# A decoder trunk in fp32: paired matmuls issued as a group, a planner with more rules, another step order, and one ratio per row in the differential softmax

## The chip, the cores and the metric

The kernel runs on one core of one Trainium2 chip. The metric is device time in microseconds (us). Engines are named as in the profile: PE is TensorE (matmuls), PEld its weight load, DVE is VectorE, ACT is ScalarE, POOL is GpSimd, SP issues the DMAs.

## What is computed

Two layers of a decoder on one sequence of 256 tokens, width 1024. Layer 0 mixes tokens by causal attention with 16 heads of 64 (its block size is 256, so the one block is the whole sequence and nothing is selected). Layer 1 uses differential attention: 8 heads, each with two score matrices and values of width 128. Behind each mixer stands an MLP of width 4096 with a squared ReLU. Each of the four sub-layers is modulated by a conditioning vector c and closed with a layer norm.

```python
mod = einsum('bd,lde->lbe', silu(c), ada_w) + ada_b
for i in range(2):
    shift1, scale1, gate1, shift2, scale2, gate2 = split(mod[i], 6)
    h = x * (1 + scale1) + shift1
    y = causal_attention(h) if i == 0 else diff_attention(h)
    x = layer_norm(ALPHA * x + (1 + gate1) * y)
    h = x * (1 + scale2) + shift2
    x = layer_norm(ALPHA * x + (1 + gate2) * (square(relu(h @ w_up[i])) @ w_down[i]))

# diff_attention, per head: s has two components, causal mask
p = softmax(s)                      # over keys
w = p[0] - lam * p[1]
o = rms_norm(w @ v, subln_g) * (1 - lambda_init)
```

## The kernel before

The 256 tokens are two blocks of 128 (b = 0, 1). All weights are read once, about 158 MB, on SP's queue. Every dense product is made of three matmuls in a rounded fp32 format: each weight tile `raw` is split into `hi` (ACT, L484) and `lo = raw - hi` (DVE, L485), each activation likewise, and PE adds hi·hi, hi·lo and lo·hi (L521 to L523, L538). There are three `raw` buffers of 1 MB, and eight `hi` and eight `lo` pieces.

The conditioning products stand on DVE: `aw`, 128 rows of `ada_w`, is loaded into one of two buffers and multiplied with silu(c) and summed in one instruction (L563), 96 times.

Attention goes by calls for two head pairs at a time (g = 0 to 3) and a block of queries b: 8 calls a layer. A scores call (`scores`, L783) takes two PSUM banks of the tag `sc`, of which there are two. Its matmuls contract over 64 rows, so each uses one row half of PE's array (64x128), and the two components `cpt` of a pair use the two halves. A call has 4 such matmuls for b = 0 and 8 for b = 1. The profile has two records for each. `softmax` masks on DVE and takes the exponential on ACT (L752). In layer 0 ACT scales each probability tile by its reciprocal sum (L847), PE transposes it (L765), ACT copies it out (L767), and the values matmuls (`attend_values_T`, L852) use the two column halves of the array (128x64). In layer 1 the second component is scaled on ACT by -lam over its sum (L805), DVE combines both (L806), and the values matmuls (L823) use the whole array. The RMS norm then scales the result on DVE (L834).

What sets the order: `PROGRAM` lists the steps (a: one conditioning row block; q, v, o, u, d: weight loads; V, Q: projections; T: transposes of queries and keys; S: a scores call with softmax; P: a values call; O: output projection; C: close with a norm; U, X, Y, D: MLP). Each step adds its instructions to one list. `Planner.forward` then goes through that list with its own costs per instruction and puts each engine's instructions in an order: of those it holds to be ready on the engine that is free first, it takes the one that stands earliest in the list.

```python
lim = t + wait_ns
pick = min([x for x in c if x[2] <= lim])
```

A scores or values matmul (`pairable`) may be followed at once by the next of the list if that is ready within 60 ns. `issue_in_order` fixes the result: each engine issues strictly in that order.

Of the kernel before, what the change touches and what calls it, by code (L numbers as in the profile page):

```python
# [15 lines left out]
F32 = mybir.dt.float32  # L16
F32R = mybir.dt.float32r
AF = mybir.ActivationFunctionType
ALU = mybir.AluOpType
# [26 lines left out]
    Q001 V000 a031 a037 a030 T001 Q000 Q011 S02 a024 a042 a022 q02 a021 T011 S03 a025 Q010 T010 T000 V010 S01  # L46
    a020 S00 Q002 T002 a044 a035 q03 S04 P02 a034 P01 P03 Q012 Q003 a046 a026 Q013 v01 a033 V011 V001 P00 a043
    P04 a045 T003 a023 S06 T012 S05 T013 S07 P06 a027 P05 G00 P07 K01 o00 O000 a040 a041 a047 o01 O001 a036 O010
    a032 N00 C000 O011 C010 u00 U000 u01 U001 X000 K00 a114 R010 u02 d00 a115 a126 a100 a113 a056 R000 a120 a121
    u04 d01 a124 U011 a110 u03 a101 a116 D000 d02 X001 a132 a053 a104 a112 a102 X011 a125 a050 U010 a137 a052  # L50
    a103 X010 a136 Y02 D001 D010 u06 a055 Y03 a151 a122 a106 d03 a051 D002 D003 a105 D011 d04 u07 Y04 u05 D004
    D012 Y06 a107 Y05 a145 D013 a111 a117 Y07 D014 a135 a142 d05 d07 a054 a133 d06 D015 D005 D006 a057 G01 D007
    N01 a156 C001 q10 D016 D017 C011 q11 Q100 T100 Q101 Q110 Q111 a141 q13 Q103 T110 S11 v10 T103 a131 a134 T101
    a123 a153 S12 T111 S10 Q113 a127 V100 P12 a143 a140 V110 a155 q12 S13 P10 F10 Q112 P11 F11 T113 a146 R011
    a154 F12 Q102 T102 o11 a144 T112 S14 S16 a150 S17 a130 v11 V111 P13 V101 P14 F13 G10 o10 P16 S15 F14 P17
    a147 R001 a152 F16 P15 F17 F15 O100 N10 O101 C100 u10 O110 O111 C110 U100 u11 u12 u13 d12 d10 X100 U101 u14
    D100 X101 d11 U110 a157 U111 K11 X110 D110 X111 u16 Y13 D111 u15 Y12 Y14 Y16 D112 K10 d14 d13 D113 d16 D101
    D102 D103 D104 u17 D114 d15 R110 Y15 G11 Y17 D105 D106 d17 D107 R100 C101 D115 E1 C111
# [110 lines left out]

class Planner:  # L170
# [3 lines left out]
    def __init__(self, ins, slots, psum_names, cost=_cost):  # L174
# [3 lines left out]
        self.costs = [cost(i, eng[k], psum_names) for k, i in enumerate(ins)]  # L178
# [51 lines left out]
    def forward(self, prio, wait_ns=0.0):  # L230
# [12 lines left out]
        dma = 0.0  # L243
        start, end = [0.0] * N, [0.0] * N
        orders = [[] for _ in range(5)]
        lastpe = -1

        def met(k, t):
            need[k] -= 1
# [921 lines left out]
```

## Time and profile before

| | |
|---|---|
| time, median of 3 runs | 650.22 us (648.86 to 650.66) |
| profiled execution | 649.94 us, its span 647.8 us |
| PE busy / DVE / ACT | 615.0 / 498.6 / 387.4 us |
| HBM read | 156.62 MB, 243 GB/s over the span |
| granted TensorE clock, mean | 0.994 |

Rows of the profile are read like this: a group row has line, engine, operation, out<-in, shapes and count, then busy us and mean ns of one, then the idle time of the engine just before and what ended it. A timeline row has start, duration and instruction. A wait row has who waited for whom, us in total, times and the longest. A row of a stretch has its bounds and length, busy time of each engine with the number of instructions, granted clock, share of the DMA engines and GB/s. Matmuls overlap in the pipeline and their ends are modelled, so a busy PE is not PE at its peak.

### The profile page before, as it was taken

The numbers are of one execution on the slowest core, as the hardware profiler recorded it, in microseconds if no ns is written. First come the engines' busy times: TensorE is split into PE (matmuls) and PEld (weight loads), VectorE is DVE, ScalarE is ACT, GpSimd is POOL, SyncE is SP. The second block draws the span as 40 slices with busy tenths as digits, with TensorE's granted clock in tenths as the row PEclk, the third lists the DMA queues.
The fourth block names the chain that finished last, engine by engine and source line by source line (L and its number), as shares of the span: only waits on it lengthen the run. The fifth ranks groups of instructions, "written<-read, shape, count | busy, mean of one in ns | idle before, by whom it ended". The sixth has DMA issues, their size and how long they took to land.

```text
span 647.8 us, 8858 instructions
## 1 busy us (share of the span) xinstructions
PE 615.0 (95%) x3148; PEld 498.2 (77%) x3148; DVE 498.6 (77%) x899; ACT 387.4 (60%) x731; POOL 27.7 (4%) x36
## 2 busy tenths in 40 slices
PE   4989999999999999999989999999999999999995
PEld 3767767776887787777877878788788888888884
DVE  5899779889979778788869979787885455646457
ACT  3547875787745463647446678686786556555530
POOL 0000000011000000000011002012100000000001
PEclk9999989999999999999999999999999999999998
DMA  8999857888979979798957757740767356555301
GB/s 292 409 344 378 303 181 257 296 266 276 321 243 383 311 247 365 269 365 314 323 178 273 253 189 271 250 165 31 252 206 253 135 194 195 196 191 180 148 0 66
DMA packets 66086, 158.25 MB, mean 244 GB/s; under 512 B 4057, under 2 KB 21370, under 8 KB 66042
## 3 DMA queue, kind: packets, MB, share of 16 engines
q1 hardware_dynamic: 66042, 157.68, 69.0%
q8 instruction: 25, 0.41, 0.2%
q14 instruction: 19, 0.16, 0.1%
HBM read 156.62 MB, written 1.05 MB: 243 GB/s over the span
## 4 chain that ended last, share of the span: by engine, by line
PE 58%; DMA 16%; DVE 15%; issue 4%; ACT 4%; POOL 2%; SPq 0%; DVEq 0%; ACTq 0%; POOLq 0%
PE ac L538 11%; DMA aw<-in_ada_w_dram 11%; PE sc L538 9%; PE mm L522 5%; PE mm L521 5%; PE mm L523 5%; DVE lo L485 5%; DVE aw L563 4%; PE mm L1069 4%; PE tp L1069 4%; DMA raw<-in_moba_w_in_dram 3%; PE sc L783 3%; ACT hi L484 2%; PE tp L1074 2%; PE mm L1074 2%
## 5 line engine op out<-in xcount | busy, mean ns | idle before, releaser
L485 DVE TENSOR_TENSOR lo<-raw,hi 128x1024 fp32r<-128x1024 f32 x196 | 231.0, 1198 | 61.4 <-ACT hi L484 59.9
L484 ACT CAST hi<-raw 128x1024 fp32r<-128x1024 f32 x196 | 199.4, 1034 | 109.2 <-PE sc L538 37.8
L563 DVE CUSTOM_DVE_ANT_0 aw<-aw,sbc,tabT 128x1024 f32<-128x1024 f32 x96 | 121.9, 1281 | 27.0 <-DMA aw<-in_ada_w_dram 26.9
L521 PE MATMUL mm<-hi,hT 128*128 128x512 f32 x224 | 91.2, 409 | 3.9 <-ACT hi L484 3.0
L522 PE MATMUL mm<-lo,hT 128*128 128x512 f32 x224 | 90.5, 405 | 0.7 <-DVE lo L485 0.7
L523 PE MATMUL mm<-hi,hT 128*128 128x512 f32 x224 | 89.4, 400 | 0.2 <-DVE hT L662 0.2
L1069 PE MATMUL mm<-hT,hi 128*128 128x512 f32 x192 | 61.3, 398 | 0.2 <-ACT hi L484 0.2
L1069 PE MATMUL tp<-hT,hi 128*128 128x512 f32 x192 | 61.0, 395 | 0.0
L538 PE MATMUL ac<-lo,sTh 128*128 128x512 f32 x160 | 50.9, 398 | 3.8 <-DVE lo L485 3.8
L521 PEld LDWEIGHTS mm<-hi,hT 128*128 128x128 f32 x224 | 42.6, 190 | 14.1 <-ACT hi L484 3.7
L538 PE MATMUL ac<-hi,sTh 128*128 128x512 f32 x160 | 50.7, 397 | 1.5 <-ACT hi L484 1.5
L538 PE MATMUL ac<-hi,sTl 128*128 128x512 f32 x160 | 51.2, 397 | 0.0
L522 PEld LDWEIGHTS mm<-lo,hT 128*128 128x128 f32 x224 | 42.7, 190 | 10.4 <-DVE lo L485 2.1
L523 PEld LDWEIGHTS mm<-hi,hT 128*128 128x128 f32 x224 | 42.6, 190 | 9.6 <-DVE hT L662 0.8
L538 PE MATMUL sc<-hi,sTl 128*128 128x512 f32 x144 | 45.8, 394 | 1.4 <-DVE sTl L1086 1.4
L538 PE MATMUL sc<-hi,sTh 128*128 128x512 f32 x144 | 46.2, 395 | 0.0
L538 PE MATMUL sc<-lo,sTh 128*128 128x512 f32 x144 | 45.8, 392 | 0.0
L1074 PEld LDWEIGHTS tp<-hT,lo 128*128 128x128 f32 x192 | 34.5, 188 | 7.5
L1074 PEld LDWEIGHTS mm<-hT,lo 128*128 128x128 f32 x192 | 34.2, 188 | 7.6 <-DVE lo L485 0.5
L538 PEld LDWEIGHTS ac<-lo,sTh 128*128 128x128 f32 x160 | 29.3, 188 | 11.7 <-DVE lo L485 5.9
L1074 PE MATMUL tp<-hT,lo 128*128 128x256 f32 x192 | 36.9, 279 | 0.0
L1074 PE MATMUL mm<-hT,lo 128*128 128x256 f32 x192 | 36.6, 280 | 0.1
(173 smaller groups left out, 898.2 us busy)
## 6 DMA issues: line engine op xcount, KB each, us to landing
aw<-in_ada_w_dram SPq DMA_DIRECT2D x96, 512.0 KB, 5.7
raw<-in_mlp_w_up_dram SPq DMA_DIRECT2D x32, 1024.0 KB, 6.3
raw<-in_mlp_w_down_dram SPq DMA_DIRECT2D x32, 1024.0 KB, 5.6
raw<-in_diff_w_in_dram SPq DMA_DIRECT2D x16, 512.0 KB, 5.2
raw<-in_moba_w_in_dram SPq DMA_DIRECT2D x24, 256.0 KB, 6.8
raw<-in_moba_w_in_dram SPq DMA_DIRECT2D x8, 512.0 KB, 6.0
raw<-in_moba_w_out_dram SPq DMA_DIRECT2D x4, 1024.0 KB, 4.9
raw<-in_diff_w_in_dram SPq DMA_DIRECT2D x4, 1024.0 KB, 5.4
```

Of the source, the lines that this page charges most:

```text
L484: act.copy(out=hi[:, :n], in_=raw_ap)
L485: vec.tensor_tensor(out=lo[:, :n], in0=raw_ap, in1=hi[:, :n], op=ALU.subtract)
L521: pe.matmul(dst, lhsT=xh, rhs=wh, start=start, stop=False)
L522: pe.matmul(dst, lhsT=xh, rhs=wl, start=False, stop=False)
L523: pe.matmul(dst, lhsT=xl, rhs=wh, start=False, stop=stop)
L538: pe.matmul(dsts[h], lhsT=a, rhs=w[:, h * 512:(h + 1) * 512], start=start and k == 0 and i == 0, stop=stop and k == n - 1 and i == 2)
L563: vec.tensor_tensor_reduce(out=aw, in0=aw, in1=sbc, scale=1.0, scalar=adab_cols(l, v)[:, j:j + 1], op0=ALU.mult, op1=ALU.add, accum_out=dst)
L783: pe.matmul(r[i, cpt][:, kb * P:(kb + 1) * P], lhsT=qk[l, b, g][rows, i, :], rhs=qk[l, kb, g][rows, 2 + i, :], start=True, stop=True)
L1069: pe.matmul(ps, lhsT=w[k][0][:, c_], rhs=x3[k], start=first, stop=last)
L1074: pe.matmul(ps[:, 0:S], lhsT=w[k][1][:, c_], rhs=x3[k][:, 0:S], start=False, stop=False)
```

## The change

The matmuls of one scores call, and of one values call in layer 0, get a group number. The planner starts a group only when everything that it needs from outside is there, and then issues nothing else on PE until the group is through. PE's costs in the planner depend on the kinds of a matmul and of the one before it (whole array, row half, column half). A transfer that starts near the end of the one before gets an extra delay in the planner. The backward pass, which was not called, goes. `PROGRAM` has another order of steps. In layer 0 a values call scales its four probability tiles first and then makes all transposes. In layer 1 the second component is no longer scaled on ACT: DVE adds it with the ratio -lam·sum0/sum1 per row, and the first sum goes into the RMS norm's factors.

```diff
 PROGRAM = """
-    Q001 V000 a031 a037 a030 T001 Q000 Q011 S02 a024 a042 a022 q02 a021 T011 S03 a025 Q010 T010 T000 V010 S01
+    Q000 a020 V000 a046 v01 V010 Q001 a100 a043 V011 a024 a036 T000 S00 a032 Q010 a023 a045 q02 P00 a040 a025
...
+def _kind(i):
+
+    t = tuple(i.tile_size)
+    if t == (128, 128):
+        return int(not i.is_transpose and "float32r" in str(i.ins[0].dtype))
+    return (2 if t[0] < 128 else 4) + int(any(i.tile_position))
...
+    def gap(self, x, paired, y):
+
+        a, b = self.kind[x], self.kind[y]
+        if a < 2:
+            return self.costs[x][0] + (92 if b >= 2 else 0), 0
+        if a // 2 == b // 2:
+            return 111 if a != b or paired else 223, 0
+        return 209 if paired else 313, (55, 105)[b] if b < 2 else 0
...
+            if not inside:
+                todo[g] -= 1
+                opened[g] = max(opened.get(g, 0.0), t)
+                if todo[g] == 0:
+                    for m in members[g]:
+                        if need[m] == 0:
+                            cand[4].append((m, opened[g]))
+                    return
...
-            pick = None
-            if e == 4 and pair[lastpe] and lastpe + 1 < N and pair[lastpe + 1]:
-                for x in c:
-                    if x[1] == lastpe + 1 and x[2] <= t + 60:
-                        pick = x
-            if pick is None:
-                lim = t + wait_ns
-                pick = min([x for x in c if x[2] <= lim])
+            if e == 4 and last is not None and togo.get(group[last]):
+                c = [x for x in c if group[x[0]] == group[last]]
+            pick = min([x for x in c if x[1] <= t])
...
-                dma = max(s + 1530, dma) + self.bytes_[k]
-                end[k] = dma + 1150
+                x = s + 1530 - dma
+                x = 850 if -1000 <= x <= 1000 else 230 if -2500 <= x < -1000 else 0
+                dma = max(s + 1530, dma) + self.bytes_[k] + x
+                end[k] = dma + 800
...
-    return o.ap[0][1] * _elems(o) / r / 16 * (8 + r * 4 * 0.0368) * 1.03
+    return o.ap[0][1] * _elems(o) / r / 16 * (8 + r * 4 * 0.0368)
...
+    @contextmanager
+    def together():
+        n = len(nc.cur_bb.bb.instructions)
+        yield
+        for i in nc.cur_bb.bb.instructions[n:]:
+            groups[i.name] = n
...
-        for i in range(2):
-            for kb in range(b + 1):
-                for cpt in (1, 0):
...
+        with together():
+            for i in range(2):
+                for kb in range(b + 1):
+                    for cpt in (1, 0):
...
-            ws = []
+            sums = small.tile([P, 4], F32, tag="sums2", name="sums2", bufs=3)
+            inv = small.tile([P, 4], F32, tag="inv", name="inv", bufs=3)
+            tt = small.tile([P, 4], F32, tag="tt", name="tt", bufs=3)
+            p1, p2 = ([softmax(b, sc[i, cpt], sums, 2 * cpt + i) for i in range(2)] for cpt in range(2))
+            vec.reciprocal(out=inv, in_=sums)
+            vec.scalar_tensor_tensor(out=tt[:, 0:2], in0=inv[:, 2:4], scalar=nlam, in1=sums[:, 0:2],
+                                     op0=ALU.mult, op1=ALU.mult)
             for i in range(2):
-                sums = small.tile([P, 2], F32, tag="sums2", name="sums2", bufs=4)
-                p1 = softmax(b, sc[i, 0], sums, 0)
-                p2 = softmax(b, sc[i, 1], sums, 1)
-                vec.reciprocal(out=sums, in_=sums)
-                vec.tensor_tensor(out=sums[:, 1:2], in0=sums[:, 1:2], in1=nlam, op=ALU.mult)
-                act.activation(out=p2[:, :n], in_=p2[:, :n], func=AF.Copy, scale=sums[:, 1:2])
-                vec.scalar_tensor_tensor(out=p1[:, :n], in0=p1[:, :n], scalar=sums[:, 0:1], in1=p2[:, :n],
+                vec.scalar_tensor_tensor(out=p1[i][:, :n], in0=p2[i][:, :n], scalar=tt[:, i:i + 1], in1=p1[i][:, :n],
                                          op0=ALU.mult, op1=ALU.add)
-                ws.append(p1)
-            probs[kind, b, g] = ws, None
+            vec.tensor_scalar(out=tt[:, 2:4], in0=inv[:, 0:2], scalar1=P ** -0.5, scalar2=None, op0=ALU.mult)
+            probs[kind, b, g] = p1, (inv, tt)
...
-                act.activation(out=sq[:, h], in_=op[:, h], func=AF.Square, scale=P ** -0.5,
-                               accum_out=sums[:, i:i + 1])
-            rsqrt_eps(sums, sums)
+                act.activation(out=sq[:, h], in_=op[:, h], func=AF.Square, scale=tt[:, 2 + i:3 + i],
+                               accum_out=ss[:, i:i + 1])
+            rsqrt_eps(ss, ss)
+            for i in range(2):
+                h = slice(i * P, (i + 1) * P)
+                vec.tensor_scalar(out=on[:, h], in0=op[:, h], scalar1=ss[:, i:i + 1], scalar2=inv[:, i:i + 1],
+                                  op0=ALU.mult, op1=ALU.mult)
...
-        for i in range(2):
-            pair = ps_[2 * i:2 * i + 2]
-            for cpt, pt in enumerate(pair):
-                c_ = 2 * i + cpt
-                act.activation(out=pt[:, :n], in_=pt[:, :n], func=AF.Copy, scale=sums[:, c_:c_ + 1])
-            pT = probs_T(b, pair)
-            for kb in range(b + 1):
...
+        for c_, pt in enumerate(ps_):
+            act.activation(out=pt[:, :n], in_=pt[:, :n], func=AF.Copy, scale=sums[:, c_:c_ + 1])
+        pT = probs_T(b, ps_)
+        with together():
+            for i in range(2):
+                for kb in range(b + 1):
...
```

How the order of instructions moves is seen at three places. (Line numbers of the changed kernel are 15 to 22 higher.)

PE in layer 0's attention, inside a scores call of block 1; `sc_624` and `sc_625` are the two banks, one for each half of the array. Before:

```order
L783 MATMUL sc_625<-qkT_541,qkT_622 128x128
L783 MATMUL sc_625<-qkT_622 128x128
L734 MATMUL tp_765<-cs_71,nat_758 128x128
L783 MATMUL sc_624<-qkT_541,qkT_622 128x128
L783 MATMUL sc_624<-qkT_622 128x128
```

And such a call now:

```order
L536 MATMUL mm_872<-hi_755,hT_101 128x512
L799 MATMUL sc_771<-qkT_609,qkT_746 128x128
L799 MATMUL sc_770<-qkT_609,qkT_746 128x128
L799 MATMUL sc_771<-qkT_746 128x128
L799 MATMUL sc_770<-qkT_746 128x128
```

The call's four matmuls into one bank stood together, then came a transpose, then the four into the other bank; now the banks alternate, and nothing stands between the call's eight matmuls.

PE at the end of layer 0's attention, where the output projection (`ac<-hi,sTh`) begins. Before:

```order
L765 MATMUL tp<-cs,p 128x128 x4
L852 MATMUL ac<-pT,v 64x128 x4
L765 MATMUL tp<-cs,p 128x128 x4
L538 MATMUL ac<-hi,sTh 128x512
L852 MATMUL mm<-pT,v 64x128 x4
L734 MATMUL tp<-cs,nat 128x128 x8
L538 MATMUL ac<-hi,sTh 128x512
```

Now:

```order
L799 MATMUL sc<-qkT 128x128 x4
L749 MATMUL tp<-cs,nat 128x128 x4
L780 MATMUL tp<-cs,p 128x128 x12
L873 MATMUL mm<-pT,v 64x128 x12
L799 MATMUL sc<-qkT 128x128 x8
L553 MATMUL ac<-hi,sTh 128x512
```

Two values calls stand together as 12 matmuls, with a scores call right behind them, and the transposes ahead.

DVE in layer 1's attention, the softmax of one scores call (`sums2`, `inv`, `tt` are the columns of sums, reciprocals and factors; `lo` rows are weight splits). Before:

```order
L803 RECIPROCAL sums2_3455<-sums2_3455 128x2
L749 ISA sc_3446,mx_3473<-sc_3446,cs_71 128x256
L749 ISA mx_3473 128x1
L804 TENSOR_TENSOR sums2_3455<-sums2_3455,nlam_513 128x1
L485 TENSOR_TENSOR lo_3717<-raw_3713,hi_3716 128x1024
L806 SCALAR_TENSOR_TENSOR p_3458<-p_3458,sums2_3455,p_3462 128x256
```

Now:

```order
L818 RECIPROCAL inv_3439<-sums2_3438 128x4
L740 TENSOR_TENSOR rtmp_3491<-mm_3465,cs_71 128x8x8
L819 SCALAR_TENSOR_TENSOR tt_3440<-inv_3439,nlam_513,sums2_3438 128x2
L824 TENSOR_SCALAR tt_3440<-inv_3439 128x2
L741 TENSOR_TENSOR rtmp_3491<-mm_3465,cs_71 128x8x8
L822 SCALAR_TENSOR_TENSOR p_3443<-p_3451,tt_3440,p_3443 128x256
```

One reciprocal serves the whole call, and the combination (L822) follows without a step on ACT in between.

More of the change, by code (lines that the diff above doesn't have):

```diff
@@ L8 @@
 import math
-from contextlib import ExitStack, nullcontext
+from contextlib import ExitStack, contextmanager
 import concourse.bass as bass
@@ L177, in __init__ @@
         eng = self.eng = [_ENG[str(i.engine).split(".")[-1]] for i in ins]
-        self.costs = [cost(i, eng[k], psum_names) for k, i in enumerate(ins)]
+        self.costs = [_cost(i, eng[k], psum_names) for k, i in enumerate(ins)]
         acc = {}
@@ L183, in __init__ @@
         self.bytes_ = [0.0] * N
-        self.pair = [eng[k] == 4 and pairable(i) for k, i in enumerate(ins)]
+        self.kind = [_kind(i) if eng[k] == 4 else 0 for k, i in enumerate(ins)]
+        self.group = [groups.get(i.name) for i in ins]
         for k, i in enumerate(ins):
@@ L239, in forward @@
         need = [len(self.preds[k]) + len(self.allocs[k]) for k in range(N)]
+        members, todo, opened = {}, {}, {}
+        for k in range(N):
+            if group[k] is not None:
+                members.setdefault(group[k], []).append(k)
+                todo[group[k]] = todo.get(group[k], 0) + len(self.allocs[k]) + sum(
+                    group[j] != group[k] for j in self.preds[k])
+        togo = {g: len(m) for g, m in members.items()}
         ready = [0.0] * N
@@ L277, in forward @@
                     if t is None or f < t:
-                        m = min([x[2] for x in c])
+                        if e2 == 4 and last is not None and togo.get(group[last]):
+                            c = [x for x in c if group[x[0]] == group[last]]
+                        m = min([x[1] for x in c])
                         if m < f:
@@ L285, in forward @@
             c = cand[e]
-            pick = None
-            if e == 4 and pair[lastpe] and lastpe + 1 < N and pair[lastpe + 1]:
-                for x in c:
-                    if x[1] == lastpe + 1 and x[2] <= t + 60:
-                        pick = x
-            if pick is None:
-                lim = t + wait_ns
-                pick = min([x for x in c if x[2] <= lim])
-            c.remove(pick)
-            k = pick[1]
-            s = pick[2] if pick[2] > free[e] else free[e]
+            if e == 4 and last is not None and togo.get(group[last]):
+                c = [x for x in c if group[x[0]] == group[last]]
+            pick = min([x for x in c if x[1] <= t])
+            cand[e].remove(pick)
+            k = pick[0]
             ii, d = costs[k]
+            f = free[e]
             if e == 4:
-                lastpe = k
-                if s > free[e] + 1 and orders[4]:
-                    ii, d = ii + 85, d + 105
+                more = 0
+                if last is not None:
+                    g, more = self.gap(last, paired, k)
+                    f = start[last] + g + hold
+                paired = kind[k] >= 2 and last is not None and kind[last] // 2 == kind[k] // 2 and kind[last] != kind[k]
+                if kind[k] >= 2:
+                    ii = 111
+                hold = more
+                if last is not None and pick[1] > f + 1:
+                    hold += 85
+                    d += 105
+                last = k
+                if group[k] is not None:
+                    togo[group[k]] -= 1
+                ii += hold
+            s = max(pick[1], f)
             free[e] = s + ii
@@ L826, in attend_values @@
         if kind == 1:
-            sums = small.tile([P, 2], F32, tag="ss", name="ss", bufs=2)
+            inv, tt = sums
+            ss = small.tile([P, 2], F32, tag="ss", name="ss", bufs=2)
             sq = ap_.tile([P, 256], F32, tag="nat", name="sq", bufs=3)
```

136 lines of the change are left out of this document (52 added, 84 removed).

## The prediction

> **What bounds the kernel now.** I read the page first (busy time by engine), then the busy time of five stretches, then the waits, and last TensorE's timeline around the scores and values matmuls that the change regroups.
>
> ```profile
> span 647.8 us, 8858 instructions
> PE 615.0 (95%) x3148; PEld 498.2 (77%) x3148; DVE 498.6 (77%) x899; ACT 387.4 (60%) x731; POOL 27.7 (4%) x36
> ```
>
> TensorE (PE) is busy for 95% of the span. Its busy time is modelled, so I look for its idle time by stage. The columns of the next view are the stretch, its length, and each engine's busy time in it (with its number of instructions), then granted clock, DMA share and GB/s. The stretches are: first products, layer 0's attention, layer 0's MLP, layer 1's attention, layer 1's MLP.
>
> ```profile
> 0.00:48.00 48.00, 36.13 (x150) 27.89 (x151) 37.64 (x74) 21.96 (x41) 0.29 (x5) 1.00 0.93 350
> 48.00:140.00 92.00, 88.95 (x517) 67.41 (x516) 76.32 (x198) 67.73 (x169) 0.00 (x0) 0.98 0.81 286
> 140.00:340.00 200.00, 190.41 (x933) 155.08 (x932) 168.46 (x232) 114.30 (x168) 7.42 (x6) 1.00 0.83 296
> 340.00:440.00 100.00, 99.95 (x543) 80.56 (x542) 87.62 (x232) 72.03 (x183) 10.57 (x14) 1.00 0.67 232
> 440.00:640.00 200.00, 199.58 (x1013) 167.24 (x1011) 124.07 (x157) 111.40 (x173) 8.49 (x10) 1.00 0.47 161
> ```
>
> The columns of engines are PE, its weight load, DVE, ACT, POOL. PE's idle time is 11.9 us in the first stretch, 3.1 in layer 0's attention, 9.6 in layer 0's MLP, and 0.5 in the 300 us after that. So in both attention stages, and in all of layer 1, PE's own work sets the pace. Only in layer 0's MLP does a second engine come near:
>
> ```profile
> ACT hi L484 <- PE sc L538: 37.8, 28, 8.1
> ACT hi L484 <- PE ac L538: 18.4, 11, 4.4
> DVE aw L563 <- DMA aw<-in_ada_w_dram: 22.2, 14, 6.2
> ```
>
> The first two rows are of the whole span: the weight split on ACT stands still for 56 us because PE has not yet freed operand buffers. Weights wait for PE, not PE for weights. The third row is of 140 to 340 us: there VectorE (DVE) waits 22.2 us for rows of the conditioning matrix. With its 168.46 us of work, DVE is taken for 190.7 of those 200 us, as long as PE is busy (190.41).
>
> **What the change does to PE's work.** A scores call has two matmuls per head pair and key block, on the two row halves of the array; a values call has pairs on the two column halves. In the trace each of these fp32 matmuls leaves two records, so a call of 4 shows as x8 and a call of 8 as x16. The same run costs very different times, by its order. Columns: start, duration, instruction.
>
> ```profile
> 69.83 1.16 PE L783 MATMUL sc<-qkT 64*128 64x128 f32 x8
> 70.91 0.33 PE L734 MATMUL tp<-cs,nat 128*128 128x128 f32 x1
> 372.84 1.16 PE L783 MATMUL sc<-qkT 64*128 64x128 f32 x16
> 373.93 0.50 PE L521 MATMUL mm<-hi,hT 128*128 128x512 f32 x1
> 378.92 0.71 PE L783 MATMUL sc<-qkT 64*128 64x128 f32 x4
> 416.71 0.72 PE L783 MATMUL sc<-qkT 64*128 64x128 f32 x8
> 433.11 1.71 PE L783 MATMUL sc<-qkT 64*128 64x128 f32 x16
> 434.75 0.73 PE L538 MATMUL ac<-hi,sTl 128*128 128x512 f32 x2
> ```
>
> The run at 372.84 alternates between the halves in the order of instructions, and its 16 records take 1.16 us. The run at 433.11 goes through one bank first, and its 16 take 1.71 us. Alternating, 8 records take 0.72 us (416.71); with one bank first, 1.16 us (69.83); and 4 records alone take 0.71 us. So two halves of a call, issued apart, pay 1.42 us for what an alternating call does in 0.72.
>
> In the new order every scores call stands as one run and alternates: 16 runs, 8 of x8 and 8 of x16, where there were 23. The values calls stand in 7 runs (three of x8, three of x16, one of x24, which is two calls), where there were 12.
>
> ```profile
> 75.96 0.66 PE L852 MATMUL ac<-pT,v 128*64 128x128 f32 x8
> 94.40 1.09 PE L852 MATMUL ac<-pT,v 128*64 128x128 f32 x16
> 48.00:140.00 92.00, 12.41 (x96) 10.01 (x96) 0.98 0.81 286
> 340.00:440.00 100.00, 10.49 (x96) 8.38 (x96) 1.00 0.67 232
> 48.00:140.00 92.00, 7.99 (x96) 4.96 (x96) 0.98 0.81 286
> ```
>
> The last three rows are busy time by stage of one line alone: scores (L783) in the two attention stages, then values (L852) in the first; the first number after the length is PE. Per layer the new scores take 4 x 0.72 + 4 x 1.16 = 7.52 us. That is 4.89 less in layer 0 and 2.97 less in layer 1. Values take 3 x 0.66 + 3 x 1.09 + 1.52 (an estimate: 1.09 plus the 0.43 between the two rows) = 6.77 us, 1.22 less. **Sum: 9.1 us of PE work, 6.1 of it before 140 us.**
>
> **What of it reaches the end.** The 3.0 us of layer 1 count in full: PE is idle for 0.05 us in that stage, and for 0.42 behind it. DVE, at 87.62 us there, fits into 97. The 6.1 us of layer 0 leave a stage of about 86 us, in which DVE has 76.32 and ACT 67.73 us of work. That still fits, and the order of DVE's instructions supports it: 37 conditioning products and 36 weight splits stand ahead of the first layer norm in both orders, and 82 and 100 ahead of the second. No work moved over these borders. But DVE is then 89% taken, and some hidden waits will show. The bounds are nothing and the whole 6.1. I take 2.5 as lost, near the 3.1 us of idle time that the stage has now.
>
> **The stall at 80 us.** One wait of PE in that stage costs more than its length.
>
> ```profile
> 80.13 0.40 PE L523 MATMUL mm<-hi,hT 128*128 128x512 f32 x1
> 82.12 0.71 PE L783 MATMUL sc<-qkT 64*128 64x128 f32 x4 [1.59 <-ACT p L752]
> 84.00:87.40 3.40, 3.40 (x10) 2.71 (x10) 2.48 (x11) 0.83 (x1) 0.00 (x0) 0.57 0.60 167
> ```
>
> The scores call waits 1.59 us until the softmax before it has freed its banks, and soon after the granted clock is 0.57 for 3.40 us, which loses 3.40 x 0.43 = 1.5 us. That is 3.1 together. A new order puts other work there. The bounds: all 3.1 gained, or a second such event, 3.1 lost. I take a gain of 1.5, since the group rule lets a call start only when all its inputs are there, but PE still follows a fixed order.
>
> **Step order and the planner's new transfer costs.** They change no instruction's cost, only when things are late. What they could win is PE's 9.6 us of idle time in 140 to 340 us. What they could lose I bound by the same amount. I take 0, as the rows ahead of the norms are the same in number. The first 48 us keep their order but for a few transfers: 0. The last 8 us, behind the last matmul, are as they were: 0.
>
> **One ratio per row** (layer 1's softmax).
>
> ```profile
> L805 ACT ACTIVATE p<-p,sums 128x256 f32<-128x256 f32 (+1 forms) x16 | 7.3, 458 | 1.9 <-DVE sums L804 1.9
> L834 DVE TENSOR_TENSOR on<-mm,ss 128x256 f32<-128x256 f32 x4 | 1.7, 424 | 0.6 <-POOL ss L612 0.5
> L727 DVE TENSOR_TENSOR nat<-nat,rtmp 128x128 f32<-128x128 f32 x16 | 4.5, 283 | 0.0
> L803 DVE RECIPROCAL sums<-sums 128x2 f32<-128x2 f32 x16 | 2.6, 162 | 1.1 <-ACT p L752 1.0
> ```
>
> ACT loses 16 scalings, 7.3 us. DVE loses 16 small reciprocals and 16 small products (32 x about 0.16 us) and 8 scalings of 256 columns (8 x 0.424), 8.5 us in all. It gains 24 small operations (3.9 us) and 16 scalings of 128 columns. Their form is not in the trace; by the nearest row, 283 ns, they take 4.5 us, and 424 ns each would be the upper bound, 6.8. So DVE is about even (0 to 2.3 us more). Both engines lie under PE there (72.03 and 87.62 against 99.95 us), so I cost this at 0; without that cover it would be at most 2.3 us. The chain from exponential to transposes loses one ACT step, but waits for four exponentials where it waited for two. In layer 0 the four scalings now stand before all transposes of a call. ACT has 24 us free in that stage, so that is 0 too.
>
> **Sum.** The profiled execution took 649.94 us, its span 647.8 and 2.1 around it. 649.9 - 9.1 + 2.5 - 1.5 = 641.8. The median of the runs is 650.22, which is 0.3 above the profiled one, so I forecast 642.
>
> **Rivals.**
> *The gain of layer 0 is given back (17%).* If DVE with its waits for conditioning rows sets the pace from 140 to 340 us (190.7 of 200 us), PE only arrives there earlier and waits longer. Then layer 1's 3.0 us remain: 646.9. For it speaks that sum of 190.7. Against it, PE is just as full in that stage, and the 56 us that the splits wait for PE.
>
> *The clock falls (13%).* In the new order one stretch at the end of layer 0's attention holds 4 scores, 16 transposes, 12 values and 8 scores matmuls with no dense matmul between them. The trace shows one fall of the clock, after a wait among such short runs. Each more costs 1.5 us by the row above. With one stall like that at 80 us kept and one clock fall added, the time is 641.8 + 1.5 + 1.5, about 645.
> [...]
>
> *The runs do not pair up (5%).* Then 8 records cost 1.16 and 16 cost 1.71 us. Scores would be 2 x (4 x 1.16 + 4 x 1.71) = 22.96 us against 22.90 now, and the 1.2 of values is lost in waits: about 650. Against it speak three alternating runs that the trace already has.
>
> *Conditioning rows come later (10%), the slower end.* The place is L563 in 140 to 340 us. DVE goes through its instructions in order, so a product that waits for its transfer holds the splits behind it, and PE waits for those. Now 22.2 us of such waits stand beside 9.6 us of idle PE, 0.43 for one. If the new order doubles the waits, the end moves by 9.6 us: 649.9 - 9.1 + 2.5 + 9.6, about 653. It outweighs the gain from 21 us of more waits on. Against it: the same number of these products stands ahead of each norm as before.
>
> **How the numbers follow.** The forecast has 55%, with a range of its own of 637 to 646. The low end is 649.9 - 9.1 - 3.1 and half of the 9.6 us: 633. The high end takes in the clock, the give-back and the unpaired runs: 650. A measurement of this kernel tells about 0.3% (2 us) from no change. Faster by more: forecast, give-back and clock, 85% less 2 for their tails, 83%. Within: the unpaired runs and tails, 8%. Slower: 9%.
>
> **What would show it.** Scores busy near 15.0 us in all and values near 6.8; x16 runs of 1.16 and x8 runs of 0.72 us everywhere; PE idle below 5 us in layer 0's attention; clock at 1.00 there. The forecast is wrong if the scores runs still take 1.71 us, or if PE's idle time in layer 0's MLP grows by more than 5 us while DVE's waits at its L563 line grow.

## The result, and the profile after

The changed kernel takes 633.31 us (median of 4 runs, 632.71 to 635.73), the kernel before beside it 650.29 us (648.86 to 650.66). The ratio is 0.975, with a 95% interval of 0.972 to 0.9779. That is 17 us less, where I had forecast 8. The time lies inside my range of 633 to 650, but at its very edge, and below the forecast's own range of 637 to 646. The sign was right and the size was half.

The head of the profile after:

```profile
span 630.5 us, 8816 instructions
PE 603.7 (96%) x3148; PEld 493.3 (78%) x3148; DVE 501.2 (79%) x899; ACT 383.0 (61%) x711; POOL 21.7 (3%) x36
```

PE is busy for 11.3 us less than before, while the span is 17.3 us shorter. So part of the gain is not PE's work at all but time in which PE stood still. The chain of waits says the same. Its shares by engine, first before, then after:

```profile
PE 58%; DMA 16%; DVE 15%; issue 4%; ACT 4%; POOL 2%; SPq 0%; DVEq 0%; ACTq 0%; POOLq 0%
```

```profile
PE 83%; DMA 7%; DVE 6%; issue 1%; POOL 1%; ACT 1%; SPq 1%; DVEq 0%; ACTq 0%; POOLq 0%
```

Before, 31% of the chain went through DMA and DVE. I made no use of this view in the prediction, though it pointed at the answer. A chain that ends last and leaves PE for 42% of its length is not that of a kernel bound by PE alone.

The five stretches of the kernel after. The columns are those of the prediction's table of stretches, with the bounds moved to the shorter stages:

```profile
0.00:48.00 48.00, 36.65 (x150) 28.24 (x151) 37.68 (x74) 22.81 (x44) 0.29 (x5) 1.00 0.93 345
48.00:134.00 86.00, 82.97 (x524) 64.07 (x523) 77.94 (x199) 68.51 (x164) 2.54 (x2) 1.00 0.86 313
134.00:322.00 188.00, 184.42 (x911) 153.40 (x909) 164.65 (x230) 109.75 (x162) 4.95 (x4) 0.99 0.86 309
322.00:425.00 103.00, 102.68 (x567) 82.80 (x568) 92.19 (x235) 70.80 (x176) 8.90 (x16) 1.00 0.68 233
425.00:623.00 198.00, 197.02 (x1000) 164.77 (x998) 124.52 (x159) 111.15 (x167) 4.14 (x8) 1.00 0.47 162
```

For a comparison the bounds have to be at the same work. I take the places where PE transposes the normed rows of block 1 (L654 before, L669 after): behind layer 0's attention at 156.5 us before and 150.5 after, and behind layer 0's MLP at 338.0 and 322. Between them PE does nearly the same number of matmuls. First the kernel before, then the one after, each with layer 0's attention and layer 0's MLP:

```profile
48.00:156.50 108.50, 104.67 (x585) 79.04 (x583) 91.69 (x222) 79.46 (x187) 5.02 (x4) 0.98 0.79 276
156.50:338.00 181.50, 172.74 (x851) 141.78 (x850) 151.08 (x207) 100.64 (x144) 2.40 (x2) 1.00 0.85 302
```

```profile
48.00:150.50 102.50, 96.25 (x579) 74.39 (x579) 93.98 (x228) 77.71 (x180) 5.09 (x4) 0.98 0.87 312
150.50:322.00 171.50, 171.14 (x856) 143.09 (x854) 148.62 (x201) 100.55 (x146) 2.40 (x2) 1.00 0.86 309
```

Layer 0's MLP goes from 181.5 to 171.5 us with five more matmul records in it. PE is idle there for 0.4 us instead of 8.8. I had put this stage at 0. With each dense matmul that moved over a bound counted at 0.235 us (half of the 0.47 us from 129.69 to 130.16 us in the trace of the kernel after, where two of them start), the 17.3 us by which the last matmul ends sooner divide so: layer 0's attention 4.6, **layer 0's MLP 11.2**, layer 1 1.5.

The waits in 150.5 to 322 us of the kernel after (who waits for whom, us in total, times, longest):

```profile
ACT hi L499 <- PE sc L553: 27.1, 14, 9.2
ACT hi L499 <- PE tp L1091: 16.4, 12, 4.2
DVE aw L578 <- DMA aw<-in_ada_w_dram: 6.6, 4, 3.5
```

DVE's waits for conditioning rows, 22.2 us in that stage before, are 6.6 now. In their place the weight splits on ACT wait for PE: 43.5 us in these two rows.

How a wait for rows reached PE is seen in the kernel before, in DVE's rows and then PE's:

```profile
303.70 1.28 DVE L563 CUSTOM_DVE_ANT_0 aw<-aw,sbc,tabT 128x1024 f32<-128x1024 f32 x1 [1.72 <-DMA aw<-in_ada_w_dram]
306.05 1.28 DVE L1086 TENSOR_TENSOR sTl<-nat,sTh 128x512 fp32r<-128x512 f32 x2
...
306.79 0.72 PE L538 MATMUL sc<-hi,sTl 128*128 128x512 f32 x2 [1.39 <-DVE sTl L1086]
```

DVE stands 1.72 us for its rows, the split of activations `sTl` is queued behind the product, and PE waits 1.39 us for that split. Four of PE's waits in that stage end with a split that DVE made behind such a stand. They are 4.6 of PE's 8.8 us of idle time.

### The profile page after: what moved, and what is told of

It reads as the page before. It is cut to its first block, busy times and chain, and to the rows that moved or that the text cites. A ratio compares the mean times of both kernels' runs of the same rounds, so it can differ in the third digit from the quotient of the medians.

```text
span 630.5 us, 8816 instructions
## 1 busy us (share of the span) xinstructions
PE 603.7 (96%) x3148; PEld 493.3 (78%) x3148; DVE 501.2 (79%) x899; ACT 383.0 (61%) x711; POOL 21.7 (3%) x36
## 4 chain that ended last, share of the span: by engine, by line
PE 83%; DMA 7%; DVE 6%; issue 1%; POOL 1%; ACT 1%; SPq 1%; DVEq 0%; ACTq 0%; POOLq 0%
PE ac L553 18%; PE sc L553 12%; PE mm L1091 7%; PE tp L1091 7%; PE mm L536 7%; PE mm L538 7%; PE mm L537 7%; PE mm L1096 4%; PE tp L1096 4%; DMA raw<-in_moba_w_in_dram 3%; DMA aw<-in_ada_w_dram 2%; PE sc L799 2%; DVE lo L500 1%; PE tp L780 1%; PE tp L749 1%
## 5 line engine op out<-in xcount | busy, mean ns | idle before, releaser
L537 PEld LDWEIGHTS mm<-lo,hT 128*128 128x128 f32 x224 | 42.6, 190 | 11.2 <-DVE lo L500 3.0
L553 PEld LDWEIGHTS ac<-hi,sTh 128*128 128x128 f32 x160 | 29.5, 188 | 6.9 <-ACT hi L499 0.6
```

The source lines that it names most:

```text
L537: pe.matmul(dst, lhsT=xh, rhs=wl, start=False, stop=False)
L553: pe.matmul(dsts[h], lhsT=a, rhs=w[:, h * 512:(h + 1) * 512], start=start and k == 0 and i == 0, stop=stop and k == n - 1 and i == 2)
```

## What the regrouping did

Busy time of the scores (L799) in the two attention stages, then of the values (L873), in the kernel after:

```profile
48.00:135.00 87.00, 7.55 (x96) 6.02 (x96) 1.00 0.86 312
330.00:425.00 95.00, 7.74 (x96) 6.21 (x96) 1.00 0.65 225
48.00:135.00 87.00, 7.01 (x96) 5.08 (x96) 1.00 0.86 312
```

Scores are 15.29 us (predicted 15.04, before 22.90), values 7.01 (predicted 6.77, before 7.99). Single runs, in the timeline of the kernel after:

```profile
59.71 0.71 PE L799 MATMUL sc<-qkT 64*128 64x128 f32 x8
100.05 1.16 PE L799 MATMUL sc<-qkT 64*128 64x128 f32 x16
409.64 1.39 PE L799 MATMUL sc<-qkT 64*128 64x128 f32 x16
```

All x8 runs and seven of the eight x16 runs are as predicted; the one at 409.64 is not, and I did not find out why. Counted from the start of the matmul ahead to the start of the one behind, less the usual step of the former, all these runs took 35.6 us in 35 pieces before and 23.9 in 23 pieces now: 11.7 less. This count holds the waits inside the runs, and what PE loses on entering and leaving one.

The stall at 80 us is gone, but another one stands at the end of layer 0's attention. PE's rows, ACT's and DVE's in the timeline of the kernel after, and then a stretch of 3.40 us behind it:

```profile
139.21 0.62 PE L553 MATMUL sc<-hi,sTl 128*128 128x512 f32 x2
142.89 0.80 PE L536 MATMUL mm<-hi,hT 128*128 128x512 f32 x1 [3.06 <-ACT hT L676]
...
140.48 1.85 ACT L673 ACTIVATE full<-tp,B,A 128x128 f32<-128x128 f32 x5 [2.30 <-DVE B L596]
...
137.95 1.27 DVE L578 CUSTOM_DVE_ANT_0 aw<-aw,sbc,tabT 128x1024 f32<-128x1024 f32 x1
139.15 1.22 DVE L500 TENSOR_TENSOR lo<-raw,hi 128x1024 fp32r<-128x1024 f32 x1
140.29 0.16 DVE L596 TENSOR_TENSOR B<-B,col 128x8 f32<-128x8 f32 x1
```

```profile
142.30:145.70 3.40, 2.81 (x7) 2.15 (x8) 3.40 (x6) 3.40 (x8) 0.00 (x0) 0.50 1.04 373
```

The normed rows are ready, but their modulation needs the column B, and its last conditioning product only starts at 137.95. PE waits 3.06 us, and the granted clock is 0.50 for 3.40 us. PE is busy for 2.81 of these, so I estimate the loss by the clock at 2.81 x 0.50, 1.4 us more.

## Experiments

Each kernel was timed against the one before in three rounds on one chip, in three sessions on three chips. Ratios are to the kernel before, with their 95% intervals. Set against the changed kernel, the kernels below stand 1 to 3 us higher by their medians than by these ratios.

**Order inside a run.** The changed kernel, in which each scores run goes through one bank first:

```diff
     p.forward()
+    o, res, n = p.orders[4], [], 0
+    while n < len(o):
+        m = n
...
+        run = o[n:m + 1]
+        if p.kind[run[0]] in (2, 3):
+            run = [k for k in run if p.kind[k] == 3] + [k for k in run if p.kind[k] == 2]
...
```

> The changed kernel with one difference: inside each of the 16 scores runs the matmuls of one bank come first and then those of the other; everything else keeps its place. If PE's own work sets the pace (theory 1), scores busy goes from about 15 to about 23 us (8 x 1.16 + 8 x 1.71), and the time rises by nearly all of the 7.9 us, to about 641. If scores time was hidden behind other engines and the gain came from the step order alone (rival), it stays within 2 us of 633.

Measured: 639.17 us, 0.9815 [0.977, 0.9859]. That is 5.9 us above the changed kernel by the medians, 4.2 by the ratios. Two scores runs of its timeline:

```profile
62.58 0.72 PE L810 MATMUL sc<-qkT 64*128 64x128 f32 x8
117.02 1.71 PE L810 MATMUL sc<-qkT 64*128 64x128 f32 x16
```

Only the runs of 16 records cost more. A run of 8, four records to one half and four to the other, is as fast as an alternating one. So the 1.16 us that I had read at 69.83 for 8 records "with one bank first" was not the price of that order: that run was half of a call of 16, split by a transpose. Its profiled execution has a span 7.3 us longer than the changed kernel's. Of that, 2.9 us are there before its first scores run, though PE, DVE and ACT have the changed kernel's order: the granted clock was 0.51 in 39.70 to 43.10 us and 0.50 in 56.80 to 60.20, and 1.00 in the changed kernel's same two stretches. So these 2.9 us are no effect of the edit. The runs themselves take 28.0 us instead of 23.9. So about 4 us of the gain hang on alternating, and not nearly all of the 7.9 that I expected.

**Groups.** The changed kernel, whose planner knows no groups:

```diff
-    issue_in_order(tc, ins, plan_issue(ins, slots, psum_names, groups))
+    issue_in_order(tc, ins, plan_issue(ins, slots, psum_names, {}))
```

> The changed kernel without the groups: the planner may put other matmuls into a call. In the order that results, 5 of 8 short scores calls are split in two and 2 of the 8 long ones go bank by bank, a third partly. By the rows of before that is about 20.0 us of scores against 15.0, so theory 1 expects 638 to 639. If the groups' work saving is given back elsewhere (rival): 633 to 635.

Measured: 645.8 us, 0.9923 [0.9897, 0.9949], above what both sides expected. The groups are worth 12.5 us with this step list and these transfer costs, more than the 9.1 I had for all of the regrouping. In its trace about 9 us lie in layer 0 and 4 in layer 1. The timeline at one call shows the part that I had not priced:

```profile
111.37 0.71 PE L799 MATMUL sc<-qkT 64*128 64x128 f32 x4 [1.43 <-ACT p L767]
112.92 0.71 PE L799 MATMUL sc<-qkT 64*128 64x128 f32 x4 [0.84 <-ACT p L767]
114.03 1.54 PE L780 MATMUL tp<-cs,p 128*128 128x128 f32 x6 [0.40 <-ACT p L866]
116.13 0.69 PE L780 MATMUL tp<-cs,p 128*128 128x128 f32 x2 [0.57 <-ACT p L866]
```

This call, begun before both its banks were free, stopped PE twice for exponentials, and what followed was late as well: 3.2 us of waits in these four rows, and a granted clock of 0.60 over 112 to 122 us.

**The new step list in the kernel before**, with its planner and softmax as they were:

```diff
 PROGRAM = """
-    Q001 V000 a031 a037 a030 T001 Q000 Q011 S02 a024 a042 a022 q02 a021 T011 S03 a025 Q010 T010 T000 V010 S01
...
+    Q000 a020 V000 a046 v01 V010 Q001 a100 a043 V011 a024 a036 T000 S00 a032 Q010 a023 a045 q02 P00 a040 a025
...
```

> The kernel of before with the new step list alone: old planner, no groups, old softmax. Theory 2 expects the waits for conditioning rows near 9 us and a time of about 640 (650 less 7 for the waits, and about 3 because the old planner happens to alternate more of the scores runs in this order: 7 of the 8 long calls). The rival (new costs of the planner are what counts) expects waits of 20 us or more and 646 to 649.

Measured: 651.46 us, 1.0013 [0.9996, 1.0031]: no gain alone, and slower than both sides expected. But the stages moved. Layer 0's MLP, from norm to norm, is 171.7 us long in its trace (181.5 before), and layer 0's attention is 8 us longer. PE in its timeline, in that attention:

```profile
115.36 1.17 PE L783 MATMUL sc<-qkT 64*128 64x128 f32 x8 [1.73 <-ACT p L752]
118.93 1.33 PE L765 MATMUL tp<-cs,p 128*128 128x128 f32 x5 [2.40 <-ACT p L847]
```

The list alone wins the 10 us in the MLP, and loses 8 of them in layer 0's attention, 4.1 at these two waits. So its worth cannot be read alone.

**The earlier step list in the changed kernel** (the same exchange, the other way round):

> The changed kernel with the step list of before: groups, planner costs and the ratio per row stay. Theory 2 (the step order took away DVE's waits for conditioning rows in layer 0's MLP, and with them 6 to 7 us of PE idle time there) expects those waits near 20 us again and a time of 640 to 642. The rival (the planner's new costs alone took them away) expects 633 to 636 with waits below 10 us.

Measured: 641.14 us, 0.9852 [0.9822, 0.9882]. The list is worth 7.8 us here. The waits for conditioning rows are 12.0 us in all (8.5 in the changed kernel), far from the 26.9 of the kernel before. So something other than the list has taken most of them away. In its trace layer 0's MLP has only 0.6 us of idle PE, and the attention ahead of it is 4.4 us longer than in the changed kernel.

**The earlier transfer costs in the changed kernel's planner:**

```diff
-                x = s + 1530 - dma
-                x = 850 if -1000 <= x <= 1000 else 230 if -2500 <= x < -1000 else 0
-                dma = max(s + 1530, dma) + self.bytes_[k] + x
-                end[k] = dma + 800
+                dma = max(s + 1530, dma) + self.bytes_[k]
+                end[k] = dma + 1150
...
-    return o.ap[0][1] * _elems(o) / r / 16 * (8 + r * 4 * 0.0368)
+    return o.ap[0][1] * _elems(o) / r / 16 * (8 + r * 4 * 0.0368) * 1.03
```

> The changed kernel with the planner's old costs for transfers (no extra lateness, 3% more for the bytes, 1150 ns to land). The new steps alone (on the old planner) and the new planner alone (on the old steps) each took about 10 us off layer 0's MLP. If the new steps suffice for that stage, the time stays within 3 us of 633. If the new transfer costs are needed to keep the gain, the waits for conditioning rows return and it is 638 or more.

Measured: 645.46 us, 0.9917 [0.9889, 0.9946]. The new costs are worth 12.2 us: about 6.5 in layer 0's attention and 5 in its MLP. The waits for conditioning rows come back in part: 15.5 us in all.

**Both the earlier list and the earlier transfer costs:**

> The changed kernel with both the earlier step list and the earlier transfer costs: of the change only the groups, PE's costs by kind of matmul, and the ratio are left. Earlier runs: the old list alone costs 7.8 us, the old transfer costs alone 12 us. Theory (the two serve the same thing, transfers that the planner holds to have landed too early, so their losses overlap): 643 to 649 us, and waits of DVE for conditioning rows of 18 us or more. Rival (they add up): 651 to 655 us, so that all of the change's gain would hang on them.

Measured: 644.25 us, 0.9885 [0.9844, 0.9926]. The losses of 7.8 and 12.2 us overlap to 10.9, and waits for conditioning rows are back at 33.3 us. Both numbers are as the theory had them, but its reason holds for the waits alone. In layer 0's MLP either part suffices: the waits are 9.3 us without the new list, 11.0 without the new costs and 22.9 without both. In the time the two need each other: with the old costs the new list wins nothing (645.46 us against 644.25 with the old one), and with the new costs it wins 7.8 (633.31 against 641.14). What is left, groups, PE's costs by kind and softmax, is worth about 7 us on the old list. PE's costs by kind and the other order inside layer 0's values calls were not tried alone.

**Conditioning rows believed to land sooner.** This asks whether those waits cost time. Only the planner's belief changes, so that it puts the products too early into DVE's order. It makes the whole order anew with that belief, so other things can move too:

```diff
                 end[k] = dma + 800
+                if str(getattr(getattr(getattr(self.ins[k].outs[0], "bass_ap", None), "tensor", None), "name", "")).startswith("aw"):
+                    end[k] -= 1500
```

> The changed kernel, in which the planner alone holds each transfer of conditioning rows to land 1.5 us sooner; no other cost changes. Theory (DVE that waits for conditioning rows holds weight splits, and those hold PE): waits of DVE at that product go from 8.5 to 18 us or more, PE's idle time in layer 0's MLP from 0.4 to 4 us or more, and the time is 637 us or more. Rival (these waits lie beside PE's work, and what the old transfer costs lost was lost through weight tiles): the waits grow as much, PE stays idle for under 2 us there, and the time is under 636 us.

Measured: 657.87 us, 1.0079 [1.005, 1.0108]. One wrong number for one kind of transfer undoes all of the change and ends 0.8% above the kernel before. Its layer 0's MLP, and the wait there:

```profile
162.90:347.00 184.10, 175.25 (x847) 143.54 (x847) 153.51 (x211) 99.71 (x144) 2.40 (x2) 0.98 0.86 303
```

```profile
DVE aw L580 <- DMA aw<-in_ada_w_dram: 21.5, 14, 6.4
```

With 21.5 us of such waits PE is idle for 8.9 us, nearly the numbers of the kernel before (22.2 and 8.8). The chain is the one seen there, DVE's rows and then PE's:

```profile
324.26 1.28 DVE L580 CUSTOM_DVE_ANT_0 aw<-aw,sbc,tabT 128x1024 f32<-128x1024 f32 x1 [6.38 <-DMA aw<-in_ada_w_dram]
328.94 1.28 DVE L580 CUSTOM_DVE_ANT_0 aw<-aw,sbc,tabT 128x1024 f32<-128x1024 f32 x1 [1.02 <-DMA aw<-in_ada_w_dram]
331.29 1.29 DVE L1110 TENSOR_TENSOR sTl<-nat,sTh 128x512 fp32r<-128x512 f32 x2
...
332.03 0.73 PE L555 MATMUL ac<-hi,sTl 128*128 128x512 f32 x2 [2.70 <-DVE sTl L1110]
```

DVE stands for 6.38 us before one product and 1.02 before another. The split of activations `sTl` is queued behind them, and PE waits 2.70 us for it. This stage holds 12.6 of the 25.7 us by which the span is longer than the changed kernel's. Another 12.4 arise ahead of it, and this run does not show that they come from the same waits.

**Weight tiles believed to land sooner**, the same edit for the transfers of `raw`:

> The changed kernel, in which the planner alone holds each weight tile to land 1.5 us sooner; no other cost changes. Theory that conditioning rows are what counts: under 636 us, PE idle for under 2 us in layer 0's MLP. Rival (weight tiles that are held to be there too soon stop ACT and DVE at their splits, and then PE): 637 us or more, with 4 us or more of idle PE in layer 0's MLP and waits of ACT's splits for transfers that the changed kernel does not have.

Measured: 640.22 us, 0.9818 [0.9785, 0.985]. Layer 0's MLP, then PE's longest wait in layer 0's attention and the end of DVE's queue ahead of it:

```profile
157.00:328.30 171.30, 170.19 (x849) 142.16 (x849) 147.52 (x200) 99.98 (x144) 2.40 (x2) 1.00 0.86 309
```

```profile
100.61 0.17 DVE L813 RECIPROCAL sums<-sums 128x4 f32<-128x4 f32 x1
...
101.27 0.33 PE L782 MATMUL tp<-cs,p 128*128 128x128 f32 x1 [4.13 <-ACT p L868]
```

The loss is real, as the rival had it, but at neither theory's place. Layer 0's MLP is as short as in the changed kernel, with 1.1 us of idle PE. The cost sits in the attention, where splits and conditioning products on DVE stand ahead of a softmax's reciprocal, and PE waits 4.13 us for the probabilities. ACT's splits wait 21.9 us for layer 0's projection weights, 14.0 in the changed kernel.

**Taking the waits away with a third buffer** for conditioning rows. The memory for it came from one `hi` buffer, so a control without that buffer goes with it; both start from the kernel before:

```diff
-        hi = wp.tile([P, 1024], F32R, tag="hi", name="hi", bufs=8)
+        hi = wp.tile([P, 1024], F32R, tag="hi", name="hi", bufs=7)
...
-        ada_rows(l, v, j, cl[:, j:j + 1], "aw", 2)
+        ada_rows(l, v, j, cl[:, j:j + 1], "aw", 3)
```

> Control for the next run: the kernel of before with seven hi buffers where it had eight (this frees 4 KB a partition). The planner makes its order anew. Expected: 650 to 654, waits of DVE for conditioning rows near 20 us in layer 0's MLP, and PE idle there for 9 to 11 us.

> The control with the freed 4 KB given to a third buffer for conditioning rows, so that their loads start one product earlier. If those waits are what makes PE idle in layer 0's MLP (theory 2), the waits fall below 8 us, PE's idle time there falls to 4 us or less, and the time is 6 to 9 us below the control. If they only stand beside it (rival: the stage is short of split weights, whatever the rows do), the waits fall, but the time stays within 2 us of the control.

Measured: the control takes 683.37 us, 1.0496 [1.0427, 1.0565], and with the third buffer 678.46, 1.042 [1.039, 1.0451]. The waits fall from 21.0 to 9.7 us in all, and from 16.4 to 8.1 in layer 0's MLP. But that stage stays at 189.3 and 188.1 us, with PE idle for 9.8 and 8.6, so little is won there. The time fell by 4.9 us, with overlapping intervals, which is between what the two sides expected. This speaks for the rival, though less than it would with eight buffers: the control alone lost 32 us, and a kernel that is held up so much elsewhere says little about a smaller limit. No run had both a third buffer and eight `hi` buffers, so taking the waits away with eight was not tried.

**The new stall.** The changed kernel with one conditioning step (`a100`) moved behind layer 0's attention, so that DVE comes to B's products sooner:

```diff
-    Q000 a020 V000 a046 v01 V010 Q001 a100 a043 V011 a024 a036 T000 S00 a032 Q010 a023 a045 q02 P00 a040 a025
+    Q000 a020 V000 a046 v01 V010 Q001 a043 V011 a024 a036 T000 S00 a032 Q010 a023 a045 q02 P00 a040 a025
...
-    O001 C000 O010 O011 u01 U001 a137 C010 a141 X001 a056 K11 u00 a113 u03 K00 a050 a153 a150 U000 a103 X000
+    O001 C000 O010 O011 u01 U001 a100 a137 C010 a141 X001 a056 K11 u00 a113 u03 K00 a050 a153 a150 U000 a103 X000
```

> The changed kernel with one step moved: the one conditioning block of layer 1 that stands near the start of the list (a100) goes behind layer 0's attention. After the change PE stands still for 3.06 us at 139.8 us, until the shift columns of the first norm are there, and then runs 3.4 us at half clock. DVE does the last six conditioning products ahead of these columns in 16 us, so one less should bring them 1 to 3 us sooner. Expected: that wait below 1.5 us, the clock's fall gone, 629 to 631. Rival (DVE is held by weight splits there, not by products): 633 plus or minus 1.

Measured: 632.62 us, 0.972 [0.9688, 0.9752], against 0.975 [0.972, 0.9779]: not to be told from the changed kernel. The wait of 3.06 us shrinks to 0.73 and the granted clock is 1.00 there (140 to 148 us), but other short waits and an order with more matmuls ahead of the norm take its place. This stall, as plain as it was in the trace, was not money on the table.

**The earlier softmax and RMS norm in layer 1:**

```diff
             for i in range(2):
...
+                vec.reciprocal(out=sums, in_=sums)
+                vec.tensor_tensor(out=sums[:, 1:2], in0=sums[:, 1:2], in1=nlam, op=ALU.mult)
+                act.activation(out=p2[:, :n], in_=p2[:, :n], func=AF.Copy, scale=sums[:, 1:2])
...
```

> The changed kernel with the earlier softmax and RMS norm of layer 1: the second component is scaled on ACT, and two reciprocals and two small products stand where one ratio was. Theory (my prediction's step: worth 0, 2.3 us at most): the time is 632 to 635 us, ACT's busy time grows by about 7 us, and PE stays idle for under 1 us in layer 1's attention. Rival (the shorter chain from exponential to transposes is what keeps PE busy there): PE waits in layer 1's attention grow by 2 us or more, and the time is 636 us or more.

Measured: 637.19 us (635.35 to 639.17), 0.9774 [0.9736, 0.9812]. The median is 3.9 us above the changed kernel's, 1.6 by the ratios, and their intervals overlap. ACT's busy time grows by 4.7 us, and PE is idle for 0.6 us in layer 1's attention, near what the theory had. The profiled execution, the slowest of these runs, is 6.5 us behind the changed kernel's. Of that, 4.2 arise in layer 0, where PE, DVE and ACT have the same order, and so are no effect of the edit. The other 2.2 arise behind layer 1's attention, at a wait of PE for the split of normed activations, 1.85 us long, with a granted clock of 0.51 after it (448.50 to 451.90 us):

```profile
447.96 0.50 PE L538 MATMUL mm<-hi,hT 128*128 128x512 f32 x1 [1.85 <-DVE hT L677]
```

DVE and ACT have another order from layer 1's attention on. Inside that attention no wait of PE is longer than 0.3 us, so the softmax chain itself is not what holds PE.

## Layer 0's MLP over all the runs

From the waits and the stretches of each trace, between the same two norms, in us. The number of PE's records is given since a few matmuls move over the bounds.

| kernel | DVE waits for conditioning rows | PE idle | length | records |
|---|---|---|---|---|
| before | 22.2 | 8.8 | 181.5 | 851 |
| old list and old transfer costs | 22.9 | 6.8 | 178.7 | 847 |
| conditioning rows believed sooner | 21.5 | 8.9 | 184.1 | 847 |
| old transfer costs | 11.0 | 2.1 | 176.4 | 855 |
| new list in the kernel before | 9.7 | 0.9 | 171.7 | 850 |
| old list | 9.3 | 0.6 | 175.1 | 869 |
| no groups | 9.1 | 0.8 | 171.3 | 852 |
| after | 6.6 | 0.4 | 171.5 | 856 |
| one conditioning step moved | 7.6 | 0.7 | 170.9 | 849 |
| weight tiles believed sooner | 5.6 | 1.1 | 171.3 | 849 |
| one bank first | 5.4 | 0.5 | 171.7 | 857 |
| earlier softmax and RMS norm | 5.2 | 0.5 | 171.8 | 857 |
| before, seven `hi` buffers | 16.4 | 9.8 | 189.3 | 880 |
| the same, third buffer for rows | 8.1 | 8.6 | 188.1 | 880 |

Of the kernels with eight `hi` buffers, the three with over 20 us of waits have 7 to 9 us of idle PE; with 11 us or less it is about 2 or less. So among them the relation is not a share, as in my price of 0.43 us for one: the first ten microseconds of waits are nearly free, and of what lies beyond them more than half comes through. The two kernels with seven `hi` buffers do not follow it. There PE is as idle with 8.1 us of these waits as others are with 22, so they are one way to idle PE and not the only one. (The granted clock is 0.99 in the stretch of the old transfer costs, 0.98 in that of the rows believed sooner and 1.00 in all the others, and the row of the old list has 13 records more than the kernel after; both add to the length without idle time.)

## Why the prediction came out as it did

**PE's work (−9.1).** Right in kind and size: 8.6 us of busy time, by the runs that were marked as its sign. Pairing is a cause, as the bank-first kernel shows (4.1 us back in the runs). My price for 8 records in bank-first order was wrong. The sum did not use it, but the rival of unpaired runs did: its 22.96 us of scores would have been 19.4 by the rows of the bank-first kernel (8 of 0.72 and 8 of 1.71). What the step left out are the waits inside a split call and what PE loses on entering and leaving it once more: so counted, the runs fell by 11.7, 3.1 more than their busy time. The two parts were not told apart.

**Lost again in layer 0's attention (+2.5), and the stall at 80 us (−1.5).** With 6.1 us of work these steps gave −5.1 for the stage. Measured −4.6, which is near, by other parts. The runs there gave 8.75 with their waits, and 4.1 went elsewhere. The new stall at 139 us alone costs about 4.5, 3.06 and the 1.4 estimated for the clock, where the fall of the clock behind the old one (0.51 in 83.50 to 86.90 us, PE busy throughout) cost 1.7 by the same estimate. "PE idle below 5 us" in that stage holds in 48 to 134 us (3.0) but not up to the norm (6.3), and the clock was 0.98 up to there. One event moved from the middle of the stage to its end.

**Step order and the planner's new transfer costs (0).** This is the step that failed, and the forecast's miss is nearly all in it: measured −11.2 in layer 0's MLP. My reason was that as many conditioning products stand ahead of each norm as before. That count says which stage pays for a product, not whether its rows are there when DVE reaches it, and it was the second that moved: 22.2 us of waits became 6.6. Either the list or the costs alone shortens the stage, to 171.7 us (the list in the kernel before) and 175.1 (the costs with the old list, 13 records more); with groups and neither it is 178.7. I had the place, the row and the mechanism in hand (the slower rival uses them, with waits doubled), but let the mechanism run in one direction only. Even the bound was too small: 9.6 us of idle PE were not all there was to win, since PE's busy time also shrank, by 1.6 us with five more records. About half of PE's idle time there came through DVE's waits for rows, as the timeline of the kernel before shows; for the rest the cause stays open.

That the time still lies in the range is luck. Its low end of 633 took 9.2 us for layer 0's attention and 4.8 for its MLP, where 4.6 and 11.2 came: two errors that nearly cancel.

**Layer 1 (−3.0 in full).** Measured −1.5. Its runs did save 2.95. About 0.9 us went into short waits of dense matmuls, most of them near the first norm behind the attention, at 440 us. The remaining half microsecond I did not place.

**One ratio per row (0).** Not settled. Without it the median is 3.9 us higher, with overlapping intervals, and the profiled executions differ by 2.2 us at a place behind layer 1's attention. If it is real, it is a gain that my bounds, 0 to 2.3 us of loss, did not hold.

**The rivals.** The gain of layer 0 was not given back; conditioning rows came sooner, not later. The mechanism of that slower rival is seen in the run with rows believed sooner, which ended on its side: 657.87 us. The fall of the clock came true at one place, after a wait of 3.06 us, not in the stretch of short matmuls that I had named, where it was 1.00 (106.62 to 114.16 us).

## What to carry to other kernels

Here two engines worked in a fixed order and both were nearly full: in layer 0's MLP before, PE was busy for 172.7 of 181.5 us, and DVE was busy for 151.1 and waited 22.2 for rows. Waits inside the second one's queue reached the first. Such waits must be priced in both directions. Read the chain of waits before calling such a kernel bound by its busiest engine. A planner that held the conditioning rows to land 1.5 us sooner cost 24.6 us here; its landing times deserve measuring as much as its instruction costs. And parts that work on one order are not to be added: the new list won nothing alone, nothing beside the groups with the old transfer costs, and nearly 8 us with the new ones.

## What the hardware showed that I had not expected

*Nearly the same wait, and different clocks behind it.* The kernel with the earlier softmax and the changed kernel have the same matmuls at 53 us, and nearly the same wait. The first one's row and the granted clock 1.8 us later (last columns but two), then the second one's:

```profile
55.20 0.50 PE L537 MATMUL mm<-lo,hT 128*128 128x512 f32 x1 [1.14 <-DVE lo L500]
```

```profile
57.00:60.40 3.40, 3.40 (x12) 2.65 (x11) 2.76 (x4) 1.99 (x2) 0.00 (x0) 0.64 1.07 398
```

```profile
55.42 0.50 PE L537 MATMUL mm<-lo,hT 128*128 128x512 f32 x1 [1.15 <-DVE lo L500]
```

```profile
57.00:60.40 3.40, 3.40 (x22) 2.54 (x20) 2.97 (x4) 2.02 (x3) 0.00 (x0) 1.00 1.06 397
```

1.14 us of waiting was followed by a clock of 0.64 in these 3.40 us, while it stayed at 1.00 after 1.15 us: 12 records against 22. The bank-first kernel has this wait too, 1.15 us at 56.65, and there the clock was 0.50 behind it (56.80 to 60.20 us). What decides between them no run shows. By an estimate (3.40 us x 0.36 and x 0.50) one such fall is worth 1.2 to 1.7 us here, and the two in the bank-first kernel ahead of its first scores run stand beside 2.9 us. So differences of this size between two of these profiles may be nothing but that.

*One of eight `hi` buffers was worth 32 us* (650.97 us beside it, 683.37 with seven). With seven, ACT's weight splits wait 111 us for PE in their four largest rows, 82 with eight, and PE is idle for 52.0 us of its span instead of 32.8. How the one leads to the other was not traced.
